# Attention over 64 heads: queries and keys of the first pairs loaded and cast ahead of later values, and another set of eight groups on the vector engine

## The chip, the cores and the metric

The kernel runs on one core of a Trainium2 chip. The metric is device time in microseconds (us) of one execution. The core has five engines that run side by side, each with its own instruction stream in order: TensorE (PE; its weight loads are shown as PEld), VectorE (DVE), ScalarE (ACT), GpSimd (POOL) and SyncE (SP), which here only issues DMAs. Engines wait for each other through semaphores.

## The reference

```python
batch, heads, seq, dim = 8, 8, 512, 64        # q, k, v: float32, standard normal
scale = 1.0 / np.sqrt(q.shape[-1])
scores = np.einsum('bhqd,bhkd->bhqk', q, k) * scale
scores = scores - scores.max(axis=-1, keepdims=True)
attn = np.exp(scores)
attn = attn / attn.sum(axis=-1, keepdims=True)
return np.einsum('bhqk,bhkd->bhqd', attn, v).astype(np.float32)
```

The kernel leaves the maximum out (the scaled scores are small enough for float16 exponentials), and takes the row sum from a column of ones beside the values.

## The kernel before

**Tiling.** The 64 heads are handled as 32 pairs `g`. For each pair 256 KB of `k`, of `q` and of `v` are loaded (`load`), cast from float32 to float16 (`cast`, nearly always on POOL: lines L332 for queries and keys into `qkp`, L326 for values into `vps`), and the queries and keys are transposed on TensorE (`transposes`, L383, two parts of four matmuls) and copied out of PSUM by DVE (`copy`, L392) into `tqk`. A pair has eight blocks of scores (four chunks `c` of 128 keys, two heads). Blocks go two by two, so that there are 129 groups `m`: groups 0 to 3 are pair 0, groups 4g to 4g+3 are pair g, and the last two groups are single blocks. `scores` (L415) puts a group into one of three PSUM tiles `st`; ACT turns it into exponentials `pt` (L420). When both heads' exponentials of all four chunks are there, `values` (L504) multiplies them with the values: eight *units* of four accumulating matmuls for each pair, seven units to a PSUM bank, which DVE divides by the row sums (`normalise`, the reciprocal L479 and the product L481, called "norm" in the plan) into `ring`, from where SP stores it (L490).

**Eight groups without ACT.** The groups listed in `ON_DVE` take their exponentials on DVE by a polynomial: `raise_` reads the scores out of PSUM (`z`, L437), then five passes follow from SBUF to SBUF (`m` L453, three `y` and `pd`, all L465). Between them DVE does the copies and norms of other pairs, so that the values of a pair with such a group can only be multiplied long after the pair's other groups are done.

**PSUM.** Besides the three `st` tiles there are two banks, `x0` and `x1`, shared by transposes and values. Transposes give theirs back when `copy` has read it, values when norm has.

**The order of the work.** `Plan` writes one order for TensorE, DVE and ACT before anything runs, by stepping through time with fixed costs for each kind of step. Only its order is used; the engines then run freely behind their semaphores. TensorE's choice is made in `step_pe`, at each moment when it is free:

```python
        backlog = self.act - t
        one, two = self.free() <= t, self.free(1) <= t
        if one and (two or backlog < self.HURRY or self.tiled):
            return self.scores(t)
        if not one and backlog < self.BACKLOG and self.free() < t + self.SOON:
            return
```

Here `free()` is when the next group may be scored (its `st` tile read, its `tqk` copied), `free(1)` the same for the one after, `tiled` says that the step before was a score. Failing that it takes transposes, at most one pair ahead, and then units of values: `values` goes through the first 14 heads of `todo` in order of pairs and takes the first whose exponentials are all planned to be done and whose values `ready_v` assumes cast (by a formula in `g` alone). If a unit begins a bank and none is free, there is no unit. On DVE (`step_dve`) a raise goes first, then whichever copy or norm became ready earliest, and a polynomial pass when nothing else is ready or would become late.

**Feeding.** With the scores of the first group of pair `g`, `feed(g)` issues the loads of pair g+6 on SP and hands out casts. Casts are emitted at once, or put in a queue `held` of at most six (`hold`; an overflow pushes out the oldest). Each `copy` and `normalise` releases one held cast and each `raise_` two (`release`), made to wait for the DVE instruction emitted just before; `needed` emits whatever is still held up to a cast that TensorE is about to use. POOL does the casts strictly in the order emitted. Loads have seven buffers for each of `k`, `q` and `v`, so a load of pair g+7 waits for the cast of pair g, and SP's queue is in order as well.

**The start.** Pair 0 has its own path (`first_pair`). Then the loads of pairs 1 to 5 are issued and the casts of pairs 1 and 2, the query of pair 1 on DVE.

Of the kernel before, what the change touches and what calls it, by code (L numbers as in the profile page):

```python
# [16 lines left out]
class Plan:  # L17
# [21 lines left out]
    FIRST_EXP = 5260  # L39
    STEP = 5  # L40
    FIRST_UNIT = 4
    ON_DVE = (6, 15, 32, 44, 58, 69, 90, 103)

    LATE_NORM, LATE_COPY, HURRY, SOON, BACKLOG = 1000, 1400, 1000, 80, 1000
    MARGIN, SLACK = 1.05, 0

    def __init__(self, groups, pairs, first):
# [37 lines left out]
    def for_dve(self, m):  # L85
        return m in self.ON_DVE

# [146 lines left out]
def kernel(  # L234
# [40 lines left out]

    HALVED = range(20, 25)
    AHEAD_FROM = 3
    NU = 56
    ring = cpool.tile([P, NU, D], FP32, name="ring")
    vps = [cpool.tile([P, 2, NI, D + 1], FP16, name=f"vp{n}") for n in range(NV)]  # L280
# [14 lines left out]
    def source(src, g):  # L295
        b, h = g // ppb, 2 * (g % ppb)
        return src[b, h : h + 2].rearrange("h (p i) d -> p h i d", i=NI)

    def load_tile(g, name):
        t = lpool.tile(  # L300
            [P, 2, NI, D],
            FP32,
            tag=f"{name}32",
            name=f"{name}32_{g}",
            bufs=7,
        )
        raw.setdefault(g, {})[name] = t
        return t

    def load(g, names):  # L310
        if g >= NP:
            return
        for name in names:
            src = {"q": q, "k": k, "v": v}[name]
            t = load_tile(g, name)
            if name == "v" and g in HALVED:
                for h in range(2):
                    nc.sync.dma_start(out=t[:, h], in_=source(src, g)[:, h])
                continue
            nc.sync.dma_start(out=t[:, :, :, :], in_=source(src, g))  # L320

    def cast(g, name):
        if g >= NP:
            return
        if name == "v":
            return nc.gpsimd.tensor_copy(  # L326
                out=vps[g % NV][:, :, :, 0:D], in_=raw[g]["v"][:, :, :, :]
            )
        if g not in qkp:
            qkp[g] = qpool.tile([P, 2, NI, P], FP16, tag="qkp", name=f"qkp_{g}")  # L330
        eng = nc.vector if (g, name) == (1, "q") else nc.gpsimd
        return eng.tensor_copy(  # L332
            out=qkp[g][:, "qk".index(name)].rearrange("p i (h d) -> p h i d", h=2),
            in_=raw[g][name][:, :, :, :],
        )
# [18 lines left out]
    def hold(g, names):  # L354
        held.extend((g, name) for name in names if g < NP)
        while len(held) > 6:
            cast(*held.pop(0))
# [4 lines left out]

    def feed(g):
        load(g + 6, "kqv")
        if g < AHEAD_FROM:
            for name in "kq":
                cast(g + 3, name)
            cast(g + 2, "v")
            return
        if g == AHEAD_FROM:  # L370
            hold(g + 3, "kq")
            hold(g + 2, "v")
        hold(g + 4, "kq")
        hold(g + 3, "v")

    def transposes(g, n, bank):
        if n == 0:
# [7 lines left out]
    def copy(g):  # L385
        if g == 1:
            for n in (1, 0):
                dve(nc.vector.tensor_copy(out=tqk[g][:, n], in_=tps[g][:, n].rearrange("p i c -> p (i c)")))
            return
        release()  # L390
        dve(
            nc.vector.tensor_copy(  # L392
                out=tqk[g][:, :, :], in_=tps.pop(g).rearrange("p n i c -> p n (i c)")
            )
        )
# [79 lines left out]
    def normalise(u, n):  # L475
        o, x = os[u // 7], u % 7
        rc = opool.tile([P, 7, 1], FP32, tag="rc", name=f"rc_{u}")
        release()
        nc.vector.reciprocal(out=rc[:, 0:n], in_=o[:, x : x + n, D : D + 1])  # L479
        dve(  # L480
            nc.vector.tensor_tensor(  # L481
                out=ring[:, u % NU : u % NU + n, :],
                in0=o[:, x : x + n, 0:D],
                in1=rc[:, 0:n].broadcast_to([P, n, D]),
                op=AluOp.mult,
            )
        )
        while heads and heads[0][2] + NI <= u + n:
            g, h, u0 = heads.pop(0)
            nc.sync.dma_start(  # L490
                out=source(out, g)[:, h], in_=ring[:, u0 % NU : u0 % NU + NI, :]
            )
# [50 lines left out]
    def first_loads():  # L543
        tk = load_tile(0, "k")
        tq = load_tile(0, "q")
        for h in range(2):
            nc.scalar.dma_start(out=tk[:, h], in_=source(k, 0)[:, h])
            nc.sync.dma_start(out=tq[:, h], in_=source(q, 0)[:, h])
# [94 lines left out]
    with tc.manual_schedule():  # L643
        first_loads()
        load(1, "kq")
        load(0, "v")
        for g in range(2, 6):
            load(g, "kq")
            load(g - 1, "v")
        load(5, "v")  # L650
        make_identity(nc, ident)
        for n in range(NV):
            nc.vector.memset(vps[n][:, :, :, D : D + 1], 1.0)
        first_pair()
        for g, names in ((1, "kq"), (0, "v"), (2, "kq"), (1, "v")):
            for name in names:
                cast(g, name)
        feed(0)
        do = {
            "transposes": transposes,  # L660
            "scores": scores,
            "values": values,
            "feed": feed,
            "raise": raise_,
            "copy": lambda g, b: copy(g),
            "pass": pass_,
            "norm": lambda u, n, b: normalise(u, n),
        }
        for what, *args in Plan(groups, NP, 3).run():
            do[what](*args)  # L670
# [30 lines left out]
```

## Time and profile before

| | us |
|---|---|
| median of 11 runs | 122.28 |
| lowest and highest | 121.87, 122.97 |
| the profiled execution, its own time | 121.58 |
| its span, first to last instruction | 119.8 |
| ACT busy | 112.7 (94%) |
| DVE busy | 105.0 (88%) |
| PE busy | 103.6 (86%) |
| POOL busy | 66.0 (55%) |

The span is what the profile covers; the profiled execution's own time is 1.8 us more. Spans of single instructions overlap where they are pipelined: the pace of ACT is the distance between the starts of two exponentials, not the duration of one.

### The profile page before, as it was taken

The page shows a single profiled execution, that of the slowest core. Times are in us where ns is not written, and L with a number is a line of the kernel's source. Part 1 is how long each engine was busy: PE and PEld are TensorE (multiplying, and loading weights), DVE is VectorE, ACT ScalarE, POOL GpSimd, SP SyncE. Part 2 cuts the span into 40 slices and gives each one's busy share as a digit, 9 for nine tenths or more (in the row PEclk, how much of TensorE's full clock was granted, in tenths as well). Part 3 has the DMA queues.
Part 4 walks back from the last instruction along what each step waited for, and adds up shares of the span by engine and source line. Part 5 has one row for each costly group of instructions (what it writes and reads, how often), then busy time and mean ns, then how long its engine had stood idle before and what let it go on. Part 6 is the DMA issues. An engine that isn't in the chain of part 4 may idle for free.

```text
span 119.8 us, 4004 instructions
## 1 busy us (share of the span) xinstructions
PE 103.6 (86%) x1557; PEld 65.7 (55%) x1557; DVE 105.0 (88%) x177; ACT 112.7 (94%) x125; POOL 66.0 (55%) x101
## 2 busy tenths in 40 slices
PE   7979687988899989979888879999988989799970
PEld 2645344663656645745564547565655667377550
DVE  1568999999999899989999999999999999986261
ACT  4599998999999999999999999999999999999970
POOL 2469999996994465343948433596355654210000
PEclk9999999999999999999999999999999999999996
DMA  4999999999999999999988999897999993234253
GB/s 97 300 349 383 381 381 384 383 363 357 316 315 273 350 279 312 346 304 294 346 255 270 266 319 306 247 367 255 330 334 353 347 340 113 88 95 138 90 170 95
DMA packets 35604, 33.83 MB, mean 282 GB/s; under 512 B 2688, under 2 KB 35584, under 8 KB 35584
## 3 DMA queue, kind: packets, MB, share of 16 engines
q1 hardware_dynamic: 35152, 33.24, 85.1%
q10 hardware_dynamic: 432, 0.33, 0.9%
q8 instruction: 12, 0.20, 0.7%
q14 instruction: 8, 0.07, 0.2%
HBM read 25.17 MB, written 8.39 MB: 280 GB/s over the span
## 4 chain that ended last, share of the span: by engine, by line
ACT 24%; DVE 23%; PE 20%; DMA 13%; issue 8%; SPq 7%; POOL 3%; ACTq 0%; POOLq 0%
ACT pt L420 24%; DMA v<-in_v_dram 10%; PE st L415 9%; PE o L504 8%; DVE y L465 7%; SPq L320 5%; DVE ring L481 4%; DVE tqk L392 4%; DVE z L437 3%; DMA out_dram<-ring 3%; PE tp L383 2%; DVE pd L465 2%; POOL vp L326 1%; DVE m L453 1%; DVE rc L479 1%
## 5 line engine op out<-in xcount | busy, mean ns | idle before, releaser
L420 ACT ACTIVATE pt<-st 128x1024 f16<-128x1024 f32 (+1 forms) x118 | 107.8, 1221 | 0.4 <-PE st L415 0.3
L415 PE MATMUL st<-tqk 64*128 64x512 f16 x248 | 45.1, 382 | 6.8 <-ACT pt L420 5.4
L504 PE MATMUL o<-vp,pt 128*128 128x65 f16 x944 | 42.1, 194 | 2.4 <-DVE tqk L392 1.1
L504 PEld LDWEIGHTS <-pt 128*128 128x128 f16 x944 | 36.1, 98 | 14.3 <-issue 11.5
L332 POOL CAST qkp<-k 128x512 f16<-128x512 f32 x31 | 21.5, 694 | 22.7 <-DMA out_dram<-ring 4.7
L326 POOL CAST vp<-v 128x512 f16<-128x512 f32 x32 | 26.1, 818 | 6.1 <-DVE y L465 2.4
L415 PEld LDWEIGHTS <-tqk 64*128 64x128 f16 x248 | 12.3, 93 | 21.0 <-issue 14.5
L481 DVE TENSOR_TENSOR ring<-o,rc 128x448 f32<-128x448 f32 (+2 forms) x37 | 22.6, 612 | 1.3
L332 POOL CAST qkp<-q 128x512 f16<-128x512 f32 x30 | 19.5, 648 | 7.6 <-DVE pd L465 2.3
L465 DVE SCALAR_TENSOR_TENSOR y<-y,m 128x1024 f32<-128x1024 f32 x16 | 21.6, 1353 | 0.1
L383 PE MATMUL tp<-ident,qkp 128*128 128x128 f16 x248 | 19.4, 219 | 2.1 <-DVE tqk L392 0.9
L392 DVE COPY tqk<-tp 128x1024 f16<-128x1024 f16 x30 | 20.4, 681 | 0.0
L383 PEld LDWEIGHTS <-qkp 128*128 128x128 f16 x248 | 14.3, 97 | 10.2 <-POOL qkp L332 5.0
L465 DVE SCALAR_TENSOR_TENSOR y<-m 128x1024 f32<-128x1024 uint32 x8 | 10.8, 1356 | 0.1
L479 DVE RECIPROCAL rc<-o 128x7 f32<-128x7 f32 (+2 forms) x37 | 7.2, 194 | 4.2 <-PE o L504 4.0
L437 DVE TENSOR_SCALAR z<-st 128x1024 uint32<-128x1024 f32 x8 | 9.7, 1216 | 1.0 <-PE st L415 1.0
L465 DVE SCALAR_TENSOR_TENSOR pd<-y,z 128x1024 uint32<-128x1024 f32 x8 | 10.2, 1281 | 0.0
L504 PE MATMUL o<-vp,pd 128*128 128x65 f16 x64 | 9.3, 194 | 0.2 <-DVE pd L465 0.2
L504 PEld LDWEIGHTS <-pd 128*128 128x128 f16 x64 | 6.3, 98 | 0.8 <-issue 0.5
L453 DVE TENSOR_SCALAR m<-z 128x1024 uint32<-128x1024 uint32 x8 | 6.1, 757 | 0.0
L552 PE MATMUL st_0a<-const-bfloat16-1.0 128*128 128x512 bf16 (+1 forms) x11 | 3.5, 482 | 0.8 <-PEq L685 0.8
L552 PEld LDWEIGHTS <-const-bfloat16-1.0 128*128 128x128 bf16 x15 | 1.7, 129 | 2.4 <-issue 2.4
(44 smaller groups left out, 18.9 us busy)
## 6 DMA issues: line engine op xcount, KB each, us to landing
out_dram<-ring SPq DMA_DIRECT2D x63, 128.0 KB, 4.2
k<-in_k_dram SPq DMA_DIRECT2D x31, 256.0 KB, 5.0
q<-in_q_dram SPq DMA_DIRECT2D x31, 256.0 KB, 5.2
v<-in_v_dram SPq DMA_DIRECT2D x27, 256.0 KB, 5.2
v<-in_v_dram SPq DMA_DIRECT2D x10, 128.0 KB, 4.0
k<-in_k_dram ACTq DMA_DIRECT2D x2, 128.0 KB, 2.8
q<-in_q_dram SPq DMA_DIRECT2D x2, 128.0 KB, 2.6
out_dram<-obl SPq DMA_DIRECT2D x1, 64.0 KB, 1.6
```

The source lines that it names most:

```text
L326: return nc.gpsimd.tensor_copy(out=vps[g % NV][:, :, :, 0:D], in_=raw[g]["v"][:, :, :, :])
L332: return eng.tensor_copy(out=qkp[g][:, "qk".index(name)].rearrange("p i (h d) -> p h i d", h=2), in_=raw[g][name][:, :, :, :],)
L383: nc.tensor.transpose(tps[g][:, n, i, :], qkp[g][:, n, i, :], ident)
L392: nc.vector.tensor_copy(out=tqk[g][:, :, :], in_=tps.pop(g).rearrange("p n i c -> p n (i c)"))
L415: nc.tensor.matmul(st[:, x, :], kc, qc, start=True, stop=True)
L420: nc.scalar.activation(out=pt[:, 0:size, :], in_=st[:, 0:size, :], func=EXP, scale=scale)
L437: nc.vector.tensor_scalar(out=r["z"][:, :, :], in0=r["st"][:, :, :], scalar1=scale * 1.4426950408889634 * 2.0**26, scalar2=15 * 2.0**26, o ...
L453: nc.vector.tensor_scalar(out=r["m"][:, :, :], in0=r["z"][:, :, :], scalar1=0x03FFFFFF, scalar2=0x04000000, op0=AluOp.bitwise_and, op1=Alu ...
L465: nc.vector.scalar_tensor_tensor(out=r["bits"][:, :, :] if n == 3 else r["y"][:, :, :], in0=r["m"][:, :, :] if n == 0 else r["y"][:, :, :] ...
L479: nc.vector.reciprocal(out=rc[:, 0:n], in_=o[:, x : x + n, D : D + 1])
L481: nc.vector.tensor_tensor(out=ring[:, u % NU : u % NU + n, :], in0=o[:, x : x + n, 0:D], in1=rc[:, 0:n].broadcast_to([P, n, D]), op=AluOp. ...
L504: nc.tensor.matmul(os[u // 7][:, u % 7, :], blocks[(g, c, h)][:, y * P : (y + 1) * P], vps[g % NV][:, h, c, :], start=(c == 0), stop=(c == ...
```

## The change

It changes three things. The list `ON_DVE` keeps group 6 and has other groups in the other seven places; two thresholds of the planner move, `HURRY` from 1000 to 900 and `SOON` from 80 to 150. At the start, SP issues the queries and keys of pairs 2, 3 and 4 before the values of pairs 2 and 1, and those of pair 5 before the values of pairs 3, 4 and 5. And the casts on POOL take another order: the values of pair 1 are no longer cast ahead of pair 3's queries and keys, and a table `FIRST_VALUES` says which values are cast or held by the first seven feeds, in the order 0, 2, 1, 4, 5, 3, 6, 7, 8, 9; the values of pair 3 are held by `feed(4)` instead of being cast at once by `feed(1)`. From `feed(7)` on the values follow as before. The numbers of loads, casts, matmuls, exponentials and passes are the same.

```diff
     FIRST_UNIT = 4
-    ON_DVE = (6, 15, 32, 44, 58, 69, 90, 103)
-
-    LATE_NORM, LATE_COPY, HURRY, SOON, BACKLOG = 1000, 1400, 1000, 80, 1000
+    ON_DVE = (6, 18, 28, 48, 59, 77, 91, 104)
+
+    LATE_NORM, LATE_COPY, HURRY, SOON, BACKLOG = 1000, 1400, 900, 150, 1000
...
     AHEAD_FROM = 3
+    FIRST_VALUES = {0: (), 1: (2,), 2: (1,), 3: (4,), 4: (5, 3), 5: (6, 7), 6: (8, 9)}
...
     def feed(g):
         load(g + 6, "kqv")
-        if g < AHEAD_FROM:
+        if g <= AHEAD_FROM:
             for name in "kq":
                 cast(g + 3, name)
-            cast(g + 2, "v")
-            return
-        if g == AHEAD_FROM:
-            hold(g + 3, "kq")
-            hold(g + 2, "v")
-        hold(g + 4, "kq")
-        hold(g + 3, "v")
+        if g >= AHEAD_FROM:
+            hold(g + 4, "kq")
+        for n in FIRST_VALUES.get(g, (g + 3,)):
+            if g < AHEAD_FROM:
+                cast(n, "v")
+            else:
+                hold(n, "v")
...
         load(1, "kq")
         load(0, "v")
-        for g in range(2, 6):
+
+        for g in range(2, 5):
             load(g, "kq")
-            load(g - 1, "v")
-        load(5, "v")
+        load(2, "v")
+        load(1, "v")
+        load(5, "kq")
+        for g in range(3, 6):
+            load(g, "v")
...
-        for g, names in ((1, "kq"), (0, "v"), (2, "kq"), (1, "v")):
+        for g, names in ((1, "kq"), (0, "v"), (2, "kq")):
             for name in names:
                 cast(g, name)
         feed(0)
```

## The prediction

> **What bounds the kernel now.** I read the page first, then the timeline of each engine, then the waits.
>
> ```profile
> PE 103.6 (86%) x1557; PEld 65.7 (55%) x1557; DVE 105.0 (88%) x177; ACT 112.7 (94%) x125; POOL 66.0 (55%) x101
> L420 ACT ACTIVATE pt<-st 128x1024 f16<-128x1024 f32 (+1 forms) x118 | 107.8, 1221 | 0.4 <-PE st L415 0.3
> ```
>
> ACT is the bound: once its 118 exponentials begin it has 0.4 us of shown idle. Its timeline, and the view of its tile `pt` from 34.5 to 63.2, give the pace:
>
> ```profile
> 7.90 11.29 ACT L420 ACTIVATE pt<-st 128x1024 f16<-128x1024 f32 x12
> 19.52 96.57 ACT L420 ACTIVATE pt<-st 128x1024 f16<-128x1024 f32 x106 [0.34 <-PE st L415]
> 115.01 1.08 ACT L420 ACTIVATE pt<-st 128x512 f16<-128x512 f32 x1
> ...
> L420 ACT ACTIVATE pt<-st x32: 1017/1210/1404, 34.3 to 62.4; 128x1024 f16<-128x1024 f32 x32
> ```
>
> The last row: 31 steps in 28.1 us, 0.905 us each. From 7.90 to 115.01 there are 116 full steps and a half one (0.48): 116 x 0.905 + 0.48 = 105.5 of 107.1 us. So all that order and feeding can still give is about 1.6 us, and the number of ACT groups is not changed. The largest piece is visible: 12 steps from 7.90 end at 18.8, but the next exponential (group 17) starts at 19.52. It sits just after the raise of group 15. TensorE and DVE there:
>
> ```profile
> 15.90 1.21 PE L504 MATMUL o<-vp,pt 128*128 128x65 f16 x32
> 18.55 0.61 PE L383 MATMUL tp<-ident,qkp 128*128 128x128 f16 x8 [0.76 <-DVE ring L481]
> 19.09 1.10 PE L415 MATMUL st<-tqk 64*128 64x512 f16 x6
> ...
> 16.05 1.59 DVE L465 SCALAR_TENSOR_TENSOR y<-y,m 128x1024 f32<-128x1024 f32 x1
> 17.78 0.62 DVE L481 TENSOR_TENSOR ring<-o,rc 128x448 f32<-128x448 f32 x1
> 22.70 0.85 DVE L453 TENSOR_SCALAR m<-z 128x1024 uint32<-128x1024 uint32 x1
> 51.77 1.22 DVE L465 SCALAR_TENSOR_TENSOR y<-y,m 128x1024 f32<-128x1024 f32 x1
> ```
>
> The transposes of pair 5 wait for a bank that the norm frees at 18.4, with group 17's scores queued behind them. Scores to exponential is 19.52 - 19.09 = 0.43 us. Eight units of values are 1.21 us with the tail, 0.13 each in a row. POOL and SP:
>
> ```profile
> 14.39 1.60 POOL L326 CAST vp<-v 128x512 f16<-128x512 f32 x1
> 16.50 1.60 POOL L332 CAST qkp<-q 128x512 f16<-128x512 f32 x1
> 18.61 0.61 POOL L332 CAST qkp<-k 128x512 f16<-128x512 f32 x1
> 22.96 1.07 POOL L332 CAST qkp<-k 128x512 f16<-128x512 f32 x1
> ...
> 17.49 0.37 SPq L320 DMA_DIRECT2D q<-in_q_dram  x1
> 23.60 0.37 SPq L320 DMA_DIRECT2D v<-in_v_dram  x1
> ...
> DMA to landing us min/median/max: 5.4/5.4/5.4
> ```
>
> Loads go out every 0.7 us. The first SP row is the query load of pair 8; the last row, of a view of that DMA alone, lets it land at 17.49 + 5.4 = 22.9. The cast at 14.39 is that of pair 3's values, the 23.60 row the load of pair 10's. Casts follow each other every 0.56 us, 0.62 the last, and are stretched to 1.07 or 1.60 beside a pass.
>
> **The change, part by part.**
>
> *Loads.* Pair 3's key and query move up one place, pair 4's two, pair 5's one, at 0.7 us a place; pair 1's values go back five, pair 2's one, pair 3's two; from pair 4's values on every place is as before. The earlier queries buy nothing: pair 4's transposes at 14.07 wait nearly as long for the copy that frees their bank, and ACT runs on over it; pair 5's wait for the norm at 18.4, which ends after their cast. Without these covers they would be worth at most the 1.0 us that the weight loads waited for POOL at each. Pair 1's values are not missed either, since its group 6 is on DVE until 21.4; they would be cast by 16.3.
>
> *Thresholds.* I followed the planner by hand, for its order alone. Up to group 14 one thing moves: `SOON` lets group 7's scores go ahead of a unit at 10.3. That exponential already starts without delay, so nothing. `HURRY` puts two units ahead of group 21's scores near 22.1, two exponentials before they are due: nothing. Both act later too; that goes into the bounds of the other raises.
>
> *Group 15 to ACT, group 18 to DVE.* In planner time group 15's exponential ends at 19.72. With no raise at 18.05, group 6's last pass takes its place, and pair 1 is complete at 19.48 instead of 21.24. TensorE then does: transposes 5 (18.15), scores 17 (18.80), one unit of pair 1 (19.48), scores 18 (19.72), three units, scores 19 (20.64), transposes 6, scores 20 (21.56), three units, scores 21 and 22 (22.36, 22.68), the eighth unit, and at **23.14 the values of pair 3**: the only pair complete, with a bank that copy 6 frees at 22.65. Seven units follow, and only then scores 23. The planner assumes these values cast at 15.2, a formula that the change leaves alone.
>
> *Where the cast of pair 3's values now is.* `feed(3)` holds k7 q7 v4, `feed(4)` k8 q8 v5 v3. Copy 4 and norm 7 release k7, q7; copy 5 v4; norm 14 k8; raise 18 q8 and v5; copy 6 v3. POOL is in order, so v3 stands behind q8, whose load (place unchanged) lands at 22.9. Without contention: q8, v5, v3 from 22.95, end 22.95 + 0.56 + 0.56 + 0.62 = 24.7. One cast stretched by an `m` pass (1.07, +0.45) gives 25.1; one more by a `y` pass (1.60, +1.0) 26.1. I take 25.1: the `m` pass of group 18 falls there by the order copy 6, pass, norm; the `y` pass begins only about when v3 is under way.
>
> *What waits.* TensorE reaches pair 3's first unit about 23.2 (in this stretch before, the planner's scores 22 at 23.15 ran at 23.32) and stands until 25.1. Queued behind it are seven units, 0.9 us, and scores 23, which ACT needs 0.43 us ahead: 25.1 + 0.05 + 0.9 + 0.43 = 26.5. Before, group 23's exponential starts six steps after 19.52, at 24.95. Both kernels have sent two groups past ACT by then, so the difference is the loss, with the stall at 19.52 already in it: **+1.5 us**, between +1.1 (24.7) and +2.5 (26.1).
>
> The contention row is 1.59 against 1.22 for the pass and 1.60 against 0.61 for the cast: both lose. The Trainium skill, "SBUF — State Buffer", section "Who interferes with whom", says that a vector instruction with two SBUF inputs, or in a two-port mode, and a GpSimd instruction that reads SBUF exclude each other, the later one blocked until the first is done. By that rule a cast behind a whole 1.22 us pass would lose 1.2 instead of 1.0 and the pass nothing, putting the upper end at +2.7 us; the rows show a loss on both sides.
>
> *SP.* The load of v10 (23.60 before) needs v3's buffer and goes out about 1.5 us later, with k11, q11 and later stores queued behind. Some 5 us of issued loads lie ahead of it and the casts of pair 11 come after 30; cost 0, or up to 1.5 us more on those casts if that cover is gone.
>
> *The other six moved raises.* Steps above 0.905 lie next to raises: 0.34 us in all by group 32, 0 by 44 and 58, 0.35 by 69, 0.07 by 90, 0.15 by 103; together 0.9. Of 28, 48, 59, 77, 91, 104 the trace shows nothing. None stalling is -0.9, all at 0.35 +1.2; I take 0, as the new list draws from the same kinds of place.
>
> Sum: 121.58 + 1.5 = 123.1 for the profiled execution, which is 0.7 below the median; for the median 122.28 + 1.5 = **123.8**.
>
> **Rivals.**
> 1. *Faster: the values of pair 3 are not missed.* This holds if TensorE comes to them after about 24, or if the v3 cast ends by 23.5. Then the 0.5 us at 19.52 goes, since ACT has group 15 to do while group 17's scores are late, and POOL, having no back-to-back casts around 16, gives the pass there back its 0.37. 122.28 - 0.6 = 121.7. For it: the planner's time may be early on a slowed DVE. Against: q8 cannot land before 22.9.
> 2. *No change:* the first rival's order, with raise 18 costing what raise 15 did: 122.3.
> 3. *Much slower: pair 3 is taken before pair 1,* at 19.7. It decides if group 6's last pass ends after 19.72 in the plan; I find 19.48. ACT is then fed only to 20.8 and gets scores again after 24.7 + 0.5 + 0.4: 4 to 5 us lost, 126.5.
>
> **How the numbers follow.** The forecast has 0.66, rival 1 0.19, rival 2 0.07, rival 3 0.08. A measurement of this kernel tells about 0.3%, 0.37 us, from no change: faster 0.19, same 0.07, slower 0.74. The forecast's own range is 122.28 + 1.1 - 0.9 to 122.28 + 2.5 + 1.2, 122.5 to 126.0, its ends both unlikely together; to leave out 2 in 10, the low end goes into rival 1 and the high end stops short of rival 3: 121.7 to 125.3.
>
> **What would show it.** Right: POOL's ninth L326 row or so ends near 25, TensorE waits 1.5 to 2.5 us for it near 23.2 (L504 on POOL vp), and ACT shows idle time of some 1.5 us before a start near 26.5, with no gap at 19.5. Wrong: L504 runs through 23 to 25, or the loss sits at raises 28 to 104. A wait of 5 us from 19.7 would be the third rival.

## The result, and the profile after

The changed kernel takes 123.07 us (median of 12 runs, 122.69 to 123.57) against 122.09 us for the kernel before in the 47 runs beside it: 1.0 us more, a ratio of 1.0077 with a 95% interval of 1.0057 to 1.0096. The ratio leaves out one slow execution of the kernel before, at 124.30 us. The profiled execution took 123.19 us, its span 121.4 us, 1.6 us more than in the profile of before.

The page of the changed kernel, engines and the two costliest groups that changed (out<-in, count, busy and mean, then idle before and its releaser):

```profile
PE 103.9 (86%) x1557; PEld 65.8 (54%) x1557; DVE 104.2 (86%) x177; ACT 112.7 (93%) x125; POOL 62.1 (51%) x101
L421 ACT ACTIVATE pt<-st 128x1024 f16<-128x1024 f32 (+1 forms) x118 | 107.8, 1201 | 2.2 <-PE st L416 2.0
L505 PE MATMUL o<-vp,pt 128*128 128x65 f16 x944 | 42.6, 194 | 3.2 <-POOL vp L327 2.6
```

ACT is as busy as before and still the bound, but its idle time has gone from 0.4 to 2.2 us, 2.0 of it in one piece. TensorE's values now wait 2.6 us for POOL's value casts. The changed kernel's timelines of ACT, TensorE, POOL and DVE show where (start, duration, line, count, idle before):

```profile
7.68 17.09 ACT L421 ACTIVATE pt<-st 128x1024 f16<-128x1024 f32 x18
26.75 90.92 ACT L421 ACTIVATE pt<-st 128x1024 f16<-128x1024 f32 x100 [1.98 <-PE st L416]
...
18.44 0.61 PE L384 MATMUL tp<-ident,qkp 128*128 128x128 f16 x8 [0.55 <-DVE ring L482]
25.33 1.05 PE L505 MATMUL o<-vp,pt 128*128 128x65 f16 x28 [2.20 <-POOL vp L327]
26.32 0.60 PE L416 MATMUL st<-tqk 64*128 64x512 f16 x4
...
22.57 1.02 POOL L333 CAST qkp<-k 128x512 f16<-128x512 f32 x1 [0.27 <-DVE tqk L393]
23.54 0.61 POOL L333 CAST qkp<-q 128x512 f16<-128x512 f32 x1
24.10 1.18 POOL L327 CAST vp<-v 128x512 f16<-128x512 f32 x2
...
22.44 0.68 DVE L454 TENSOR_SCALAR m<-z 128x1024 uint32<-128x1024 uint32 x1
27.20 1.22 DVE L466 SCALAR_TENSOR_TENSOR y<-m 128x1024 f32<-128x1024 uint32 x1
```

Read from POOL: pair 8's key cast is stretched to 1.02 us beside DVE's `m` pass, its query, which had landed at 23.10, follows only at 23.54, then two value casts in one row, those of pairs 5 and 3, ending at 25.28. TensorE, idle for 2.20 us, starts pair 3's 28 matmuls (seven units) 0.05 us later, and only then the scores that ACT is waiting for. Group 23's exponential starts at 26.75, that is 1.47 us after the end of the cast.

### The profile page after: what moved, and what is told of

It reads as the page before. It is cut to its first block, busy times and chain, and to the rows that moved or that the text cites. A ratio compares the mean times of both kernels' runs of the same rounds, so it can differ in the third digit from the quotient of the medians.

```text
span 121.4 us, 4004 instructions
## 1 busy us (share of the span) xinstructions
PE 103.9 (86%) x1557; PEld 65.8 (54%) x1557; DVE 104.2 (86%) x177; ACT 112.7 (93%) x125; POOL 62.1 (51%) x101
## 4 chain that ended last, share of the span: by engine, by line
PE 31%; ACT 26%; DVE 22%; issue 8%; DMA 7%; POOL 2%; SPq 1%; ACTq 0%
ACT pt L421 26%; PE o L505 14%; PE st L416 13%; DVE y L466 8%; DVE tqk L393 4%; DMA v<-in_v_dram 4%; PE tp L384 4%; DVE ring L482 4%; DMA out_dram<-ring 3%; DVE z L438 3%; DVE m L454 1%; POOL vp L327 1%; DVE rc L480 1%; DVE pd L466 1%; SPq L321 1%
## 5 line engine op out<-in xcount | busy, mean ns | idle before, releaser
L505 PE MATMUL o<-vp,pt 128*128 128x65 f16 x944 | 42.6, 194 | 3.2 <-POOL vp L327 2.6
L327 POOL CAST vp<-v 128x512 f16<-128x512 f32 x32 | 22.6, 711 | 9.3 <-DVE y L466 6.8
L333 POOL CAST qkp<-q 128x512 f16<-128x512 f32 x30 | 18.8, 627 | 13.9 <-DVE y L466 8.2
L466 DVE SCALAR_TENSOR_TENSOR y<-y,m 128x1024 f32<-128x1024 f32 x16 | 20.0, 1252 | 0.0
L466 DVE SCALAR_TENSOR_TENSOR pd<-y,z 128x1024 uint32<-128x1024 f32 x8 | 10.9, 1357 | 0.0
```

Of the source, the lines that this page charges most:

```text
L327: return nc.gpsimd.tensor_copy(out=vps[g % NV][:, :, :, 0:D], in_=raw[g]["v"][:, :, :, :])
L333: return eng.tensor_copy(out=qkp[g][:, "qk".index(name)].rearrange("p i (h d) -> p h i d", h=2), in_=raw[g][name][:, :, :, :],)
L466: nc.vector.scalar_tensor_tensor(out=r["bits"][:, :, :] if n == 3 else r["y"][:, :, :], in0=r["m"][:, :, :] if n == 0 else r["y"][:, :, :] ...
L505: nc.tensor.matmul(os[u // 7][:, u % 7, :], blocks[(g, c, h)][:, y * P : (y + 1) * P], vps[g % NV][:, h, c, :], start=(c == 0), stop=(c == ...
```

## The experiments

Times are medians; each ratio is to the kernel before in runs on the same chip (122.11 us in the first four, 122.15 us in the next four), with its 95% interval. "Group 23" is the start of that exponential, counted along ACT's timeline; in the first profile of the kernel before it was 24.96 us.

**The cast of pair 3's values moved ahead, nothing else.**

```diff
-    FIRST_VALUES = {0: (), 1: (2,), 2: (1,), 3: (4,), 4: (5, 3), 5: (6, 7), 6: (8, 9)}
+    FIRST_VALUES = {0: (), 1: (2,), 2: (1,), 3: (3,), 4: (5, 4), 5: (6, 7), 6: (8, 9)}
```

> The changed kernel with the values of pair 3 held by feed 3 and those of pair 4 by feed 4 (the two exchanged in the table), nothing else: the cast of pair 3's values stands ahead of pair 8's key and query on GpSimd and should end near 21.7 us instead of 25.3, before TensorE wants it at 23.1. My theory (the loss is TensorE's wait for that cast): the 2.0 us idle of ScalarE before group 23's exponential goes, about 121.1 to 121.6 us, faster than the kernel before. Rival (the loss comes from where the other raises stand, or from the new order of loads as such): the wait goes but the time stays within 0.4 us of the changed kernel, 122.7 to 123.4.

122.09 us, ratio 0.9976 (0.995 to 1.0003): 1.0 us less than the changed kernel and level with the kernel before. The rival falls, but the time is 0.5 us above the range that I expected. POOL and ACT of this kernel:

```profile
21.66 0.61 POOL L327 CAST vp<-v 128x512 f16<-128x512 f32 x1
...
8.26 1.02 ACT L421 ACTIVATE pt<-st 128x1024 f16<-128x1024 f32 x1
9.77 12.02 ACT L421 ACTIVATE pt<-st 128x1024 f16<-128x1024 f32 x13 [0.49 <-PE st L416]
22.24 6.53 ACT L421 ACTIVATE pt<-st 128x1024 f16<-128x1024 f32 x7 [0.45 <-PE st L416]
```

Pair 3's values are cast by 22.27 and the 2 us gap is gone. But two other stalls stand earlier, before 9.77 and before 22.24 (group 19), and group 23 starts at 25.9 instead of 24.96.

**Loads and casts alone** (the list of groups and the thresholds put back).

```diff
-    ON_DVE = (6, 18, 28, 48, 59, 77, 91, 104)
+    ON_DVE = (6, 15, 32, 44, 58, 69, 90, 103)
-    LATE_NORM, LATE_COPY, HURRY, SOON, BACKLOG = 1000, 1400, 900, 150, 1000
+    LATE_NORM, LATE_COPY, HURRY, SOON, BACKLOG = 1000, 1400, 1000, 80, 1000
```

> The changed kernel with the list of eight groups and the two thresholds of before, so loads and casts alone are changed. The values of pair 3 are then wanted only after group 15's polynomial, near 32 us. My theory: no wait for them, time within 0.4 us of before, 121.7 to 122.4. Rival (the new order of loads and casts costs by itself, for instance through later loads behind pair 10's values): 122.6 to 123.1.

122.20 us, ratio 1.0000 (0.9975 to 1.0026). The new order of loads and casts neither costs nor gains where pair 3's values are not wanted early.

**Groups and thresholds alone** (the kernel before with the two lines of the last diff the other way round).

> The kernel before with the new list of eight groups and the two new thresholds; loads and casts as before, so the values of pair 3 are cast by about 16 us. My theory: TensorE does not wait at 23.1 and the stall at 19.5 us shrinks, 121.1 to 121.8 us. Rival (the new groups cost by themselves, at raises 28 to 104): 122.6 to 123.2.

122.06 us, ratio 0.9982 (0.9953 to 1.0012). The new groups cost nothing by themselves; the gain I expected did not come either. So neither half of the change costs anything that these runs can tell, and only the two together cost 1 us.

**Group 15 in place of 18.**

```diff
-    ON_DVE = (6, 18, 28, 48, 59, 77, 91, 104)
+    ON_DVE = (6, 15, 28, 48, 59, 77, 91, 104)
```

> The changed kernel with group 15 in place of group 18 in the list, the other six new groups and the thresholds kept. Pair 3 then waits for its polynomial until about 34 us by the planner, after its values are cast. My theory: no wait near 23, so 121.5 to 122.3 us. Rival (the other six new places cost the time): 122.7 to 123.3.

122.03 us, ratio 0.9994 (0.996 to 1.0029). With pair 3 waiting for its own polynomial, its late cast is not missed. Its profiled execution had an unusually large early gap, with nothing later to swallow it: group 23 started at 26.18, and the execution took 122.67 us, 0.6 above the median:

```profile
10.04 10.19 ACT L421 ACTIVATE pt<-st 128x1024 f16<-128x1024 f32 x11 [1.29 <-PE st L416]
```

That gap follows pair 1's key, issued at 1.63 to 1.65 us in every profile and landed at 7.08 here, 5.54 in the profile of before. Four kernels without the wait at 23 thus came within 0.1 us of the kernel before, and I had expected three of them up to 1 us faster. Either the wait costs less than the profile says, or the first profile of before shows less than this kernel's usual early stalls. The next runs go after that.

**A delay of the start, with the wait at 23 and without.** Two more copies on DVE ahead of the copies of pair 1:

```diff
         if g == 1:
+            idle = wpool.tile([P, 2, S], FP16, tag="idle", name="idle", bufs=1)
+            for n in (1, 0):
+                nc.vector.tensor_copy(out=idle[:, n], in_=tps[g][:, n].rearrange("p i c -> p (i c)"))
             for n in (1, 0):
```

In the changed kernel:

> The changed kernel with two more copies of pair 1's transposes on VectorE (128x512 each, into a tile nobody reads) ahead of the two real ones near 7.5 us, about 0.76 us by the row of those copies. They delay ScalarE's group 4. Theory of absorption (the cast of pair 3's values ends when pair 8's query has landed, whatever came before, so the wait at 23 us swallows earlier delays): 123.1 to 123.4 us, within 0.3 of the changed kernel, group 23 still near 26.8 us. Rival (delays add up): 123.7 to 124.0.

122.85 us, ratio 1.0059 (1.0019 to 1.0099), no more than the changed kernel and a little below the range that I gave. The rival, a ratio of 1.0127 or more, falls. ACT:

```profile
7.71 1.05 ACT L424 ACTIVATE pt<-st 128x1024 f16<-128x1024 f32 x1
9.39 15.88 ACT L424 ACTIVATE pt<-st 128x1024 f16<-128x1024 f32 x17 [0.62 <-PE st L419]
26.70 1.94 ACT L424 ACTIVATE pt<-st 128x1024 f16<-128x1024 f32 x2 [1.42 <-PE st L419]
```

The early gap is there, the idle before group 23 has shrunk from 1.98 to 1.42 us, and group 23 starts at 26.70, as in the changed kernel. In the kernel with pair 3's values first:

> The kernel with the values of pair 3 held by feed 3 (no wait at 23 us) and the same two more copies on VectorE. Both theories: nothing is left to swallow the delay, so 0.5 to 0.9 us above that kernel's 122.1, 122.6 to 123.0 us. If it gains nothing here either, the copies are hidden elsewhere and say nothing on absorption.

122.14 us, ratio 0.9992 (0.9965 to 1.0019): a miss, the delay cost nothing here either. ACT of this kernel, then DVE of it and of the same kernel without the extra copies:

```profile
10.07 12.02 ACT L424 ACTIVATE pt<-st 128x1024 f16<-128x1024 f32 x13 [1.20 <-PE st L419]
22.29 6.53 ACT L424 ACTIVATE pt<-st 128x1024 f16<-128x1024 f32 x7 [0.19 <-PE st L419]
...
17.40 1.21 DVE L469 SCALAR_TENSOR_TENSOR y<-y,m 128x1024 f32<-128x1024 f32 x1
...
16.99 1.58 DVE L466 SCALAR_TENSOR_TENSOR y<-y,m 128x1024 f32<-128x1024 f32 x1
```

The early gap has grown to 1.20 us, but group 4 starts only 0.3 us later than without the copies (10.07 against 9.77), as this execution was ahead until then (group 3 at 7.82 against 8.26), and group 19 starts at 22.29, as it did at 22.24. The third `y` pass takes 1.21 us instead of 1.58: it now begins ahead of a cast on POOL (17.40 against 17.96), where without the copies it began behind one (16.99 against 16.89). The stall before group 19 is smaller. So early delays are partly taken back by 22 us without the wait too, and the pair of runs does not show absorption by itself; for that the starts of group 23 below are needed.

**The cast one place earlier, and three casts later.**

```diff
-    4: (5, 3)
+    4: (3, 5)
```

> The changed kernel with the values of pair 3 ahead of those of pair 5 in feed 4: one cast fewer before the one that TensorE waits for, 0.56 us earlier. My theory (the cast's end sets group 23): 122.4 to 122.7 us, TensorE's wait about 1.6 us instead of 2.2, group 23 near 26.2. Rival (another thing sets the time once the wait is shorter than some bound): as the changed kernel, 123.0, or at once as before, 122.1.

122.38 us, ratio 1.0025 (0.9995 to 1.0055): 0.6 to 0.7 us less than the changed kernel, at the edge of what I expected. The interval still holds 1, so that this run alone does not tell a shorter wait from none. The profiled execution does not show the wait that I expected, since its POOL ran ahead:

```profile
21.90 0.61 POOL L333 CAST qkp<-k 128x512 f16<-128x512 f32 x1
22.46 0.61 POOL L333 CAST qkp<-q 128x512 f16<-128x512 f32 x1
23.02 1.63 POOL L327 CAST vp<-v 128x512 f16<-128x512 f32 x2
```

Here pair 8's query landed at 22.2 instead of 23.1, its key's cast met no pass, and pair 3's values were cast by 23.6, so that group 23 started at 25.6. One place, 0.56 us, plus these two decide between a wait and none. In the other direction:

```diff
-    4: (5, 3), 5: (6, 7)
+    4: (5,), 5: (3, 6, 7)
```

> The changed kernel with the values of pair 3 held by feed 5, behind pair 9's key and query, the last of which landed at 25.2 us in the changed kernel's trace: the cast ends near 26.4 us instead of 25.3. My theory: about 1.1 us more than the changed kernel, 123.9 to 124.4 us, group 23 near 27.9. Rival (the wait is mostly hidden by other slack): within 0.4 us of the changed kernel.

125.05 us (6 runs), ratio 1.0224 (1.0175 to 1.0273). In the profiled execution, 124.43 us, TensorE's wait and group 23 are where I put them:

```profile
26.57 1.05 PE L505 MATMUL o<-vp,pt 128*128 128x65 f16 x28 [2.76 <-POOL vp L327]
...
27.99 2.86 ACT L421 ACTIVATE pt<-st 128x1024 f16<-128x1024 f32 x3 [2.55 <-PE st L416]
```

The median is 0.6 us beyond that execution and beyond my range; why the other executions lost more is open.

**The two kernels profiled again.**

> The kernel before, unchanged, profiled once more. If its first profile was a lucky one (pair 1's key landed at 5.54 us, between 5.55 and 7.08 in the other kernels), group 23 starts 0.2 to 1.0 us later than 24.96 and the execution takes 121.8 to 122.6 us. If that profile was typical, 24.9 to 25.1 us and 121.4 to 121.8.

124.15 us, group 23 at 27.5. TensorE's granted clock was 0.62 between 9 and 13 us in this execution, so it is not used to size anything. Another execution of the kernel before, in the same job, took 122.34 us.

> The changed kernel, unchanged, profiled once more. By the theory of absorption group 23 starts at the end of the cast of pair 3's values plus 1.47 us, 26.5 to 27.0 us, however late pair 1's key lands, and the execution takes 122.8 to 123.4 us. Rival (early delays add to the wait): group 23 beyond 27.1 where that key lands after 6.2.

123.32 us. ACT and TensorE:

```profile
10.05 12.02 ACT L421 ACTIVATE pt<-st 128x1024 f16<-128x1024 f32 x13 [0.68 <-PE st L416]
22.47 3.78 ACT L421 ACTIVATE pt<-st 128x1024 f16<-128x1024 f32 x4 [0.40 <-PE st L416]
26.82 1.94 ACT L421 ACTIVATE pt<-st 128x1024 f16<-128x1024 f32 x2 [0.56 <-PE st L416]
...
25.40 1.05 PE L505 MATMUL o<-vp,pt 128*128 128x65 f16 x28 [0.78 <-POOL vp L327]
```

Pair 1's key landed at 7.0 us, 1.3 later than in the first profile of this kernel. ACT lost 0.68 and 0.40 us before group 23, TensorE's wait shrank from 2.20 to 0.78 us, and group 23 started 0.07 us from where it did before. The rival, 27.1 or later, falls.

> The kernel before, unchanged, one more profile, since in the second TensorE's granted clock fell to 0.62 between 9 and 13 us. If the first profile was a lucky one, group 23 starts between 25.2 and 26.0 us and the execution takes 121.8 to 122.6 us; if it was typical, 24.9 to 25.1 us and 121.4 to 121.8.

122.00 us, near the median:

```profile
20.09 8.36 ACT L420 ACTIVATE pt<-st 128x1024 f16<-128x1024 f32 x9 [0.58 <-PE st L415]
```

Group 17 starts at 20.09 here and at 19.52 in the first profile; six steps of 0.905 us later group 23 starts at 25.52. The profile that I predicted from was 0.56 us ahead of this one.

> The kernel with the values of pair 3 held by feed 3, unchanged, profiled once more. No wait of TensorE for that cast near 23 us; group 23 starts with the early delays of that execution, between 25.0 and 26.2 us, not at the end of the cast plus 1.47.

122.20 us, group 23 at 25.8, without a wait for pair 3's values.

The starts of group 23 side by side (us; v3 stands for the cast of pair 3's values):

| kernel, profile | pair 1's key landed | TensorE's wait for v3 | group 23 | execution |
|---|---|---|---|---|
| before, first | 5.54 | none | 24.96 | 121.58 |
| before, third | 5.56 | none | 25.52 | 122.00 |
| v3 first | 6.81 | none | 25.90 | 122.33 |
| v3 first, again | 6.64 | none | 25.76 | 122.20 |
| changed, first | 5.73 | 2.20 | 26.75 | 123.19 |
| changed, again | 7.00 | 0.78 | 26.82 | 123.32 |
| changed, with delay | 5.55 | 1.6 | 26.70 | 123.16 |
| v3 in feed 5 | 6.15 | 2.76 | 27.99 | 124.43 |

In every row the execution is group 23's start plus 96.4 to 96.6 us. Of the six other profiles five agree with that, and one does not: loads and casts alone, group 23 at 25.12 and 97.0 us after it. In the four rows with the wait the start is the end of v3's cast plus 1.47 or 1.48 us. In the three of them with the cast in its place in the changed kernel that is 26.70 to 26.82, although pair 1's key landed between 5.55 and 7.00. Without the wait the start moves over almost a microsecond.

The end of v3's cast is not the same in every execution, though. The changed kernel's twelve times spread over 0.9 us, about as widely as those of the kernel before. Pair 8's key, the first of the loads behind which v3 stands, landed anywhere between 21.48 and 22.76 us in the fourteen profiles, and not in step with pair 1's key: 22.22 after 5.55, 22.35 after 7.00. By these profiles the wait swallows the early stall and puts the spread of a later load in its place.

No version tried here is measurably faster than the kernel before: the best ratios are 0.9976 and 0.9982, both with 1 inside their intervals.

## Why the prediction was right, and where its size was off

*The direction and the place* were right and are shown. TensorE finished pair 1 at 23.1 and stood before pair 3's first unit; the cast that it waited for stands where I put it, and undoing either half of the change, or exchanging two numbers in the table, takes the loss away. The order worked out by hand held: pair 1's first unit at 19.30, pair 3 after pair 1, scores 23 after seven units.

*The terms of the sum.* End of the cast 25.1 forecast, 25.28 measured; seven units and the scores 1.4 forecast, 1.47 measured; group 23 at 26.5 forecast, 26.75 measured. One cast was stretched by the `m` pass, as taken, but in this profile it was that of pair 8's key, and its end, not the landing of the query, started the row. The `y` pass came only at 27.20, behind a norm that waited for TensorE, so that the upper end of 26.1 did not arise.

*The contention* was misread. The prediction takes 1.59 against 1.22 us for the pass and 1.60 against 0.61 for the cast as one meeting in which both lose. They are two meetings, and in each the one that began first loses nothing. A line of the kernel before, then two of the changed kernel:

```profile
15.95 0.61 POOL L332 CAST qkp<-k 128x512 f16<-128x512 f32 x1
...
16.30 1.23 DVE L466 SCALAR_TENSOR_TENSOR y<-y,m 128x1024 f32<-128x1024 f32 x1
16.39 1.61 POOL L327 CAST vp<-v 128x512 f16<-128x512 f32 x1
```

Before, the cast at 15.95 keeps its 0.61 us, and the pass that begins behind it at 16.05 takes 1.59; the cast at 16.50 begins within that pass and takes 1.60. In the changed kernel the pass begins 0.09 us ahead of the cast, keeps its 1.23, and the cast alone loses. In the first profiles of both kernels all fourteen casts that began within a two-input pass took 1.47 to 1.64 us, and every such pass that met no cast under way took 1.21 to 1.23. So the rows are no evidence against the rule that the prediction sets beside them: they follow it. The bound of 26.1 does not hang on this, as it was made from the measured 1.60.

*The step that failed* is the baseline under the difference: "Before, group 23's exponential starts six steps after 19.52, at 24.95", and with it the last line of the sum, which carried the 1.5 us from one execution over to the median. The profiled execution of before lay 0.7 us below the median of the runs shown. I said so, and then added the same loss to both. But the loss is not a fixed amount: in the changed kernel group 23's start is set by when pair 8's loads land and by POOL's queue behind them, and the early stalls before it are swallowed. In the kernel before that start varies with the execution's early stalls, and 24.96 was an early one. Against the third profile's 25.52 the loss is 26.75 - 25.52 = 1.2 us, against the first's 1.8; the medians say 1.0. The term was 0.5 us too large. The sum's first line, 123.1 us for one execution, is near both the profiled 123.19 and the median 123.07, in part by luck: group 23 came 0.25 us later than forecast, and what follows it took 0.2 us less than before. The 0.7 us added to reach 123.8 is what the runs contradict. How much of it is early stalls rests on two usable profiles of the kernel before.

*The stall at 19.52* was not worth counting on. In the changed kernel it is gone from group 17, as ACT has group 15 to work on, but raise 18 has one of its own: 0.4 us of idle before group 19 in the changed kernel's second profile, 0.45 with v3 first. The second rival's mechanism, "raise 18 costing what raise 15 did", is thus what the kernels with raise 18 and without the wait show, at 122.06 and 122.09 us. The first rival's gain of 0.6 us did not appear in any of them.

*The other six moved raises* at 0: "groups alone" at ratio 0.9982 agrees. *The earlier queries* at 0: "loads and casts alone" at 1.0000 agrees. *SP's queue* was read wrongly: pair 10's values were loaded at 23.80, before the cast of pair 3's began, so that load does not wait for it: it went out 0.2 us later than before, not 1.5. The step was costed at 0 either way.

```profile
23.80 0.37 SPq L321 DMA_DIRECT2D v<-in_v_dram  x1
```

*The third rival*, a wait from 19.7, did not occur.

## What to carry to other kernels

When two parts of a schedule are drawn up separately (which pair is finished late, and in which order the inputs are prepared), check them against each other at the first consumer: here the table of casts puts pair 3 last, which suits a plan whose late pair is 3 and not one whose late pair is 4. An in-order engine makes a cast as late as the load of the cast in front of it. And a wait whose end is set by something outside, such as a landing, is worth the difference to a *typical* start of the work behind it, not to the one in a single profile: take that start from several executions before carrying a difference over to the median.

## What the runs showed of the hardware

Pair 1's key, always issued at 1.63 to 1.65 us as the first load after pair 0's, landed between 5.54 and 7.68 us in the fourteen profiles; the 7.68 belongs to the execution whose granted clock was 0.62, but only later, from 9 to 13 us. At full clock group 4's exponential stalled by up to 1.3 us with it. I had taken the start to repeat from execution to execution. The landing is not the whole of it: the first and third profiles of the kernel before have it at 5.54 and 5.56 and group 23 at 24.96 and 25.52. The spread reaches the end of the kernel except where a later wait swallows it; without one, some of it was taken back by a `y` pass that no longer began behind a cast (1.21 instead of 1.58 us).

Of a cast on POOL and a two-input pass on DVE that overlap, the one that began first kept its time and the other lost: 0.61 and 1.59 us with the cast first, 1.23 and 1.61 with the pass first.
